# A layer's first output projection, moved behind the queries and written as block products

## Chip, cores and metric

One core of a Trainium2 chip runs the whole program. The metric is the device time of one execution in microseconds (us), and the kernel before was timed three times.

## What is computed

Two layers (DEPTH = 2) are applied to x of 1024 tokens by 1024 channels, in float32. Cut to what matters here:

```python
h = rmsnorm(x, norm_g[l])
z = einsum('bld,de->ble', h, w_in[l])
u_pool, g_pool, u_lru, g_lru, q, k, v, g_attn = split(z)
y_pool = pool_mixer(u_pool, pool_w[l], pool_scale[l]) * silu(g_pool)      # 4 groups of 128 channels
y_lru  = rg_lru_bidir(u_lru, ...) * silu(g_lru)                           # 6 blocks of 128 channels
y_attn = block_attention(rope(rmsnorm(q)), rope(rmsnorm(k)), v) * silu(g_attn)   # 6 heads of 128
x = x + einsum('ble,ed->bld', concatenate([y_pool, y_lru, y_attn]), w_out[l])
```

The last line is the output projection: 2048 channels in, 1024 out. The kernel does it in two parts of eight 128-channel rows of y each: part 0 takes pool groups 0 and 1 and the six LRU blocks, part 1 the rest.

## The kernel before

**Layout and precision.** Activations lie with channels on the 128 partitions and the 1024 tokens along the free dimension. Each matmul operand is kept as two float32r tiles, the rounded value (high) and what is left (low). ScalarE (ACT) or VectorE (DVE) casts the high half, DVE subtracts it for the low one (`split_to`, 518; `fill`, 1012), and `mm3` (544) multiplies high by high, high by low and low by high: three matmuls of 128x128 by up to 512 columns.

**Order of the work.** `record_kernel` (438) writes the operations down layer by layer, and a planner (`Plan.plan`, 303) turns them into one queue for each engine. At each step it takes the operation that can start first by its own costs; among those, the lowest number wins, which is the place in the record less what `ahead(n)` (458) gives. Each engine then runs its queue in order, so an instruction that waits holds all behind it. SyncE (SP) issues the plain DMAs, GpSimd (POOL) the adding ones (`accumulate`, 515) and the `pow` of the norms.

**Buffers.** Tiles belong to groups with a fixed number of buffers (441 to 455): F has 27 of 128x1024, RAW 3 for weights as loaded, WH and WL 2 each for their high and low halves, M 5 of 128x512. A group may have to wait until another is dead (`after`): the attention tiles `at` and `ap` lie where the normalised input `hT` lay, and `st` after them. The same holds in PSUM: a layer has MM, 3 tiles of two banks, and only when all its MM tiles are dead PS, 6 tiles of one bank, in the same place; SG has the two other banks. Buffers of a group are given out in the order of the record, unless enough are free for those that stand earlier.

**A layer** (the loop at 1253): pool groups 0 and 1, six LRU blocks (each two projections of 48 matmuls, gates, scans), pool groups 2 and 3, `out_proj` (966) for part 0, then a gate projection and its silu, k and v (`phase_kv`, 832), q (`phase_q`, 878), four more gate projections, the first three score steps of the attention, the sixth gate projection, and the 48 attention steps (`att_scores`, `att_tr`, `att_pv`). The scores need a PSUM tile of MM, a row maximum on DVE, an exponential on ACT, a reciprocal and a scaling; then TensorE (PE) transposes them.

**Part 0** is a plain product: for each of 8 output tiles, 2 token halves x 8 inputs x 3 matmuls, 384 in all, with 8 weights, 8 x rows and 8 results moved by SP. Its inputs are split as soon as they are made (`lru_gate_out`, 740) and lie in F until then.

**Part 1** is already done by `Fast` (1022) in block products. The eight inputs are two rows of four tiles and the tokens two halves T1 and T2, so y is a 2x2 matrix of blocks. Seven products of each output pair, four inputs x 3 matmuls each, give what eight would: 7 x 4 x 12 = 336. For that, four sums of y blocks (t1 to t4) and, for each pair, two tiles of sums of weight blocks (`weight_sums`, 1069) are needed; the latter are made by adding DMAs in DRAM. `head` and `c11` do the products with B11 and B21 into MM tiles, `run` (1143) first t3, t2 and t4 of every pair, then t1 and B22. In layer 0 the norm of the next layer follows at once: `Norm.finish` (633) for tokens T1 is recorded between those two loops, with `ahead(-LATE)`, and its two small sums use SG.

Of the kernel before, what the change touches and what calls it, by code (L numbers as in the profile page):

```python
# [10 lines left out]
F32 = mybir.dt.float32  # L11
# [5 lines left out]
L = 2  # L17
# [33 lines left out]
DC = 300  # L51
LATE = 50

# [384 lines left out]
def record_kernel(nc, ins, outT):  # L438
# [17 lines left out]
    P.layer = 0  # L456

# [16 lines left out]
    def MM(name="mm"):  # L474
        return P.tile(f"MM{P.layer}", [128, 1024], F32, name)

    def bank(name):
        return P.tile(f"PS{P.layer}", [128, 512], F32, name)

    def SM(name="sm"):  # L480
        return P.tile("SG", [128, 512], F32, name)
# [124 lines left out]
    class Norm:  # L606
        def __init__(self, t0, cols, add="DVE", pool_lo=()):
            self.x = {}
            self.acc = None
            self.t0, self.cols, self.adder, self.pool_lo = t0, cols, add, pool_lo  # L610
            self.ss = SM("ss") if add == "PE" else None
            self.warm = None

        def add(self, xk, k=None):
# [18 lines left out]
        def finish(self, l, hT):  # L633
            t0, nc = self.t0, self.cols // 128
            r = S("nr")[:, 0:nc]
            if self.ss is None:
                ss = SM("ss")
# [12 lines left out]
            if self.warm is not None:  # L650
                self.keep_warm(self.acc, KEEP[1])
            rb = SM("rb")
            for c in range(nc):
# [311 lines left out]

    def out_proj(l, part, y, src, dst, halves, norm=None):
        xn_t = []
        for half in halves:
            t0 = half * HALF if half is not None else 0
            n = Norm(t0, HALF) if norm is not None else None  # L970
            cols = HALF if half is not None else T
            for j in range(NK):
                w = stream_w(wo[l, part, j])
                xr = RAW("xr") if half is None else M("xr")
                P.sync.dma_start(out=xr, in_=src[j][:, t0:t0 + cols])
                if half is None:
                    last = (l, part, j) == (L - 1, 1, NK - 1)
                    mm = MM()
                    parts = TAIL if last else ((0, 512), (512, 1024))
                    for a, b in parts:  # L980
                        for k in range(NK):
                            kk = slice(k * 128, (k + 1) * 128)
                            mm3(mm[:, a:b], w[0][:, kk], w[1][:, kk], y[k][0][:, a:b], y[k][1][:, a:b], k == 0, k == NK - 1)
                    for a, b in parts if last else ((0, T),):
                        P.vector.tensor_tensor(out=xr[:, a:b], in0=xr[:, a:b], in1=mm[:, a:b], op=ALU.add)
                        P.sync.dma_start(out=dst[j][:, a:b], in_=xr[:, a:b])
                else:
                    mm = MM()[:, 0:HALF]
                    proj_half(mm, w, y, half)
                    if half == 0:  # L990
                        xn_t.append(F("xn"))
                    xn = xn_t[j][:, t0:t0 + HALF]
                    P.vector.tensor_tensor(out=xn, in0=xr, in1=mm, op=ALU.add)
                    P.sync.dma_start(out=dst[j][:, t0:t0 + HALF], in_=xn)
                    n.add(xn)
            if n is not None:
                with ahead(-LATE if half == 0 else 0):
                    n.finish(*norm)

# [22 lines left out]
    class Fast:  # L1022
# [67 lines left out]

        def operand(self, src, early, sign=1):
            self.n = getattr(self, "n", -1) + 1
            w = block(("WH", "WL")[self.n % 2], "wf")
            with ahead(early):
                fill(w, src, sign)
            return w
# [46 lines left out]
        def run(self):  # L1143
# [6 lines left out]
            self.c11(*self.todo.pop(0))  # L1150
            tail = []
            for p in pairs:
# [42 lines left out]
        def c12(self, j, b, w):  # L1195
            self.product(b, w, "B22", False)
            self.add(j, T2, b, ALU.add)
            self.done(j, T2)


    P.group("Q2", 2)
    for l in range(L):
        P.group(f"ap{l}", 4, after=f"hT{l}")
    hT = alloc_hT(0)
# [48 lines left out]
    for l in range(L):  # L1253
        P.layer = l
        pw = gate_weights(wp[l])
        yp = []
        if l > 0:
            first = [stream_w(wcm[l, CH_UP]), stream_w(wcm[l, CH_GP])]
            firsts = [MM(), MM()]
            for half in range(2):  # L1260
                for w, ps in zip(first, firsts):
                    proj_half(ps[:, half * HALF:(half + 1) * HALF], w, hT, half)
        prev = pool_group(l, 0, hT, *firsts[0:2])
        cur = pool_group(l, 1, hT, *firsts[2:])
        yp.append(split(pool_out(l, 0, pw, *prev), T, "y"))
        prev = cur

        y = []
        xc = lru_conv(l, 0, proj(l, CH_UL, hT))
        yp.append(split(pool_out(l, 1, pw, *prev), T, "y"))  # L1270
        for j in range(NB):
            if j + 1 < NB:
                nxc = lru_conv(l, j + 1, proj(l, CH_UL + j + 1, hT))
            lru = Lru(l, j, gate_weights(wg[l, j]), *xc)
            lru.gates(0)
            s = silu(proj(l, CH_GL + j, hT))
            lru.gates(1)
            y.append(lru_gate_out(lru.scan(), s))
            xc = nxc
        pw = gate_weights(wp[l])  # L1280
        prev = pool_group(l, 2, hT)
        cur = pool_group(l, 3, hT)
        yp.append(pool_out(l, 2, pw, *prev, True))
        prev = cur
# [17 lines left out]
        def scores(n):  # L1302
# [5 lines left out]
            att_scores(us[i], h, kT, "F" if n < 3 else f"ap{l}")  # L1308
        scores(0)
        ws = Fast.weight_sums(l, 1, us[0].first)  # L1310
        scores(1)
        scores(2)
        sg.append(silu(proj(l, CH_GA + 5, hT, singles()), True))
        for n, (i, h) in enumerate(steps):
# [3 lines left out]
            if i > 0:  # L1318
                att_pv(us[i - 1], v, sg, h, True)
                if h == GQ - 1 and us[i - 1].g == 0 and us[i - 1].c == NT - 1:  # L1320
                    fast = Fast(l, 1, yp[2:] + sg[0:2], sg[2:6], f"st{l}", ws)
                    with ahead(-100):
# [29 lines left out]
def hymba_kernel(ctx: ExitStack, tc: tile.TileContext, *aps):  # L1352
# [12 lines left out]
    def make(t):  # L1365
# [5 lines left out]
        if g == "SG":  # L1371
            return psum.tile(t.shape, t.dtype, tag=f"{g}{t.slot}", name=t.name)
        for of, key, space in ((side, {"hT": "h", "at": "a", "ap": "a", "st": "s"}.get(g[:2]), {}),
                               (banks, {"MM": "m", "PS": "p"}.get(g[:2]), dict(space=bass.MemoryType.PSUM))):
# [86 lines left out]
```

## Time and profile before

| | us |
|---|---|
| median of 3 runs (lowest to highest) | 1629.21 (1627.88 to 1629.31) |
| the profiled execution | 1628.12 |
| its span, first to last instruction | 1626.3 |
| PE busy | 1609.0 (99%) |
| DVE busy | 1108.1 (68%) |
| ACT busy | 789.6 (49%) |
| POOL busy | 113.8 (7%) |

The span lies within the execution's time; the 1.8 us left is around it. Matmuls are pipelined, so that one has a duration of some 0.39 us and the next starts 0.23 us later: what a matmul costs in a full queue is the distance of starts, and a busy PE is one that had a matmul under way. Part 1 of layer 0 runs from 737 to 826 us and that of layer 1 from 1540 us on; part 0 of layer 0 lies within 285 to 400 us, the start of its attention at 551 us.

### The profile page before, as it was taken

The numbers are of one execution on the slowest core, as the hardware profiler recorded it, in microseconds if no ns is written. First come the engines' busy times: TensorE is split into PE (matmuls) and PEld (weight loads), VectorE is DVE, ScalarE is ACT, GpSimd is POOL, SyncE is SP. The second block draws the span as 40 slices with busy tenths as digits, with TensorE's granted clock in tenths as the row PEclk, the third lists the DMA queues.
The fourth block names the chain that finished last, engine by engine and source line by source line (L and its number), as shares of the span: only waits on it lengthen the run. The fifth ranks groups of instructions, "written<-read, shape, count | busy, mean of one in ns | idle before, by whom it ended". The sixth has DMA issues, their size and how long they took to land.

```text
span 1626.3 us, 20051 instructions
## 1 busy us (share of the span) xinstructions
PE 1609.0 (99%) x7878; PEld 1367.7 (84%) x7878; DVE 1108.1 (68%) x1675; ACT 789.6 (49%) x1262; POOL 113.8 (7%) x130
## 2 busy tenths in 40 slices
PE   8999999999999999999999999999999999999999
PEld 8788888888898889998878888888889987999987
DVE  7659889225564489998875688872255635899874
ACT  5357873012332377775342677721133325777731
POOL 1000000000121120101000000000001212101010
PEclk9999999999999999999999999999999999999999
DMA  6110111335111660107331111114431128402172
GB/s 199 39 59 33 59 39 52 127 129 187 37 39 39 181 105 20 33 5 225 113 105 51 46 57 34 62 43 147 155 128 37 40 58 201 76 17 39 32 220 97
DMA packets 51471, 136.87 MB, mean 84 GB/s; under 512 B 5936, under 2 KB 11056, under 8 KB 51248
## 3 DMA queue, kind: packets, MB, share of 16 engines
q1 hardware_dynamic: 41008, 117.88, 21.4%
q0 software_dynamic: 10368, 17.70, 6.9%
q8 instruction: 62, 1.02, 0.3%
q14 instruction: 33, 0.27, 0.1%
HBM read 109.48 MB, written 35.65 MB: 89 GB/s over the span
## 4 chain that ended last, share of the span: by engine, by line
PE 94%; DVE 2%; ACT 1%; issue 1%; DMA 1%; POOL 1%; SPq 0%; ACTq 0%; POOLq 0%
PE mm L430 62%; PE o L430 8%; PE S L430 8%; PE pt L430 5%; PE c L430 3%; PE a L430 3%; PE b L430 3%; PE d L430 1%; POOL ssq L430 1%; PE qtr L430 1%; DMA raw<-wcm 0%; DVE ra L430 0%; DVE hTl L430 0%; SPq L430 0%; DVE sq L430 0%
## 5 line engine op out<-in xcount | busy, mean ns | idle before, releaser
L430 PE MATMUL mm<-hTh,wh 128*128 128x512 f32 x784 | 309.6, 395 | 0.4 <-ACT U L430 0.4
L430 PE MATMUL mm<-hTl,wh 128*128 128x512 f32 x784 | 308.8, 394 | 0.0
L430 PE MATMUL mm<-hTh,wl 128*128 128x512 f32 x784 | 306.6, 392 | 0.0
L430 ACT CAST wh<-raw 128x1024 fp32r<-128x1024 f32 x56 | 58.8, 1050 | 291.4 <-PE mm L430 289.4
L430 PEld LDWEIGHTS mm<-hTh,wh 128*128 128x128 f32 x784 | 147.1, 188 | 35.6 <-ACT U L430 0.9
L430 PEld LDWEIGHTS mm<-hTh,wl 128*128 128x128 f32 x784 | 147.1, 188 | 34.9
L430 PEld LDWEIGHTS mm<-hTl,wh 128*128 128x128 f32 x784 | 147.3, 188 | 32.7
L430 DVE TENSOR_TENSOR wl<-raw,wh 128x1024 fp32r<-128x1024 f32 x65 | 79.2, 1220 | 95.4 <-ACT wh L430 93.1
L430 PE MATMUL mm<-wq,hTh 128*128 128x384 f32 x512 | 133.6, 341 | 0.0
L430 ACT CAST pTh<-pt 128x1024 fp32r<-128x1024 f32 x94 | 94.9, 1012 | 67.2 <-PE pt L430 67.0
L430 DVE TENSOR_TENSOR pTl<-pt,pTh 128x1024 fp32r<-128x1024 f32 x94 | 114.5, 1220 | 15.7 <-ACT pTh L430 15.2
L430 DVE TENSOR_REDUCE st<-S 128x1 f32<-128x1024 f32 x96 | 116.5, 1217 | 3.5 <-PE S L430 3.1
L430 ACT ACTIVATE p<-S,st 128x1024 f32<-128x1024 f32 x96 | 107.5, 1121 | 3.0 <-DVE st L430 3.0
L430 POOL TENSOR_TENSOR ssq<-ssq,mhalf 128x3 f32<-128x3 f32 (+1 forms) x48 | 43.5, 907 | 909.5 <-DVE ssq L430 909.5
L430 DVE TENSOR_TENSOR xr<-xr,mm 128x1024 f32<-128x1024 f32 x16 | 19.5, 1221 | 122.4 <-PE mm L430 122.4
L430 PE MATMUL mm<-yh,wh 128*128 128x512 f32 x256 | 100.8, 394 | 0.0
L430 PE MATMUL mm<-yh,wl 128*128 128x512 f32 x256 | 100.7, 393 | 0.0
L430 PE MATMUL mm<-yl,wh 128*128 128x512 f32 x256 | 100.5, 393 | 0.0
L430 PE MATMUL pt<-ident,p 128*128 128x128 f32 x752 | 97.5, 273 | 0.0
L430 PEld LDWEIGHTS pt<-ident,p 128*128 128x128 f32 x752 | 87.1, 140 | 11.0 <-ACT p L430 1.0
L430 PEld LDWEIGHTS mm<-wq,hTh 128*128 128x128 f32 x512 | 91.5, 189 | 0.0
L430 PE MATMUL o<-pTl,vh 128*128 128x384 f32 x256 | 90.2, 352 | 0.0
(188 smaller groups left out, 3313.0 us busy)
## 6 DMA issues: line engine op xcount, KB each, us to landing
raw<-wcm SPq DMA_DIRECT2D x52, 512.0 KB, 3.8
raw<-wo SPq DMA_DIRECT2D x16, 512.0 KB, 3.9
x<-xr SPq DMA_DIRECT2D x16, 512.0 KB, 2.7
wf<-w SPq DMA_DIRECT2D x16, 512.0 KB, 4.4
xn<-x SPq DMA_DIRECT2D x16, 512.0 KB, 5.5
raw<-wq SPq DMA_DIRECT2D x16, 384.0 KB, 3.3
w<-wo POOLq DMA_DIRECT2D x24, 256.0 KB, 6.8
xr<-xT SPq DMA_DIRECT2D x8, 512.0 KB, 3.7
```

What stands on the lines that cost most here:

```text
L430: getattr(real[op.engine], m)(*[res(x) for x in a], **{n: res(x) for n, x in k.items()})
```

## The change

Part 0 is no longer a plain product. The new class `First` does it in the seven block products of `Fast`, and it runs after q and all gate projections, directly before the attention. The y's go to DRAM as they are made (signed, so that the sums are additions), and the t sums of them are made there by SP copies and POOL adding DMAs; the weight sums of part 0 are made in LRU block 1. What the attention and part 1 need later (pool outputs 2 and 3 and the six silus) is stored to DRAM and loaded again behind `First`. The t blocks lie in a new group `sa`, which waits for `hT` to be dead; `at` and `ap` wait for `sa`. PSUM changes from MM to PS twice in a layer. The first three score steps are recorded inside `First`, before its last product; the sixth gate projection is no longer behind them. In part 1 of layer 0, the operands for t1 and B22 are made in the first loop and held in F, the norm's sums of the first half use PS, and LATE is 20 instead of 50; in both layers the subtraction of the t1 product is recorded with `ahead(60)`.

```diff
-LATE = 50
+LATE = 20
...
+    for i in range(2 * L):
+        P.group(f"MM{i}", 3, after=f"PS{i - 1}" if i else None)
+        P.group(f"PS{i}", 6, after=f"MM{i}")
     for l in range(L):
-        P.group(f"MM{l}", 3, after=f"PS{l - 1}" if l else None)
-        P.group(f"PS{l}", 6, after=f"MM{l}")
         P.group(f"hT{l}", 16, after=f"st{l - 1}" if l else None)
-        P.group(f"at{l}", 4, after=f"hT{l}")
+        P.group(f"sa{l}", 16, after=f"hT{l}")
+        P.group(f"at{l}", 4, after=f"sa{l}")
...
-    def lru_gate_out(h, s):
-        P.vector.tensor_tensor(out=h, in0=h, in1=s, op=ALU.mult)
-        return split(h, T, "y")
+    def lru_gate_out(h, s, signs):
+        for t, sign in zip((T1, T2), signs):
+            P.vector.scalar_tensor_tensor(out=h[:, t], in0=h[:, t], scalar=sign, in1=s[:, t], op0=ALU.mult, op1=ALU.mult)
+        return h
...
@@ Fast.run
+                if self.norm:
+                    w = self.load(self.ws[p][1])
+                    kept.append((self.operand(w[:, T1], 0, 1, "F"), self.operand(w[:, T2], 0, 1, "F")))
             self.c21(*tail.pop())
             if self.norm:
+                self.norms[0].psum = bank
                 with ahead(-LATE):
                     self.norms[0].finish(*self.norm)
             for p in pairs:
-                with ahead(150):
-                    w = self.load(self.ws[p][1])
-                    w1, w4 = self.operand(w[:, T1], 0), self.operand(w[:, T2], 0)
+                if self.norm:
+                    w1, w4 = kept[p]
+                else:
+                    with ahead(150):
+                        w = self.load(self.ws[p][1])
+                        w1, w4 = self.operand(w[:, T1], 0), self.operand(w[:, T2], 0)
                 b = bank("b") if p < 3 else SM("b")
                 self.product(b, w1, "t1", True)
-                self.add(2 * p + 1, T2, b, ALU.subtract)
+                with ahead(60):
+                    self.add(2 * p + 1, T2, b, ALU.subtract)
...
+    class First(Fast):
...
+        def put(self, k, y):
+            P.sync.dma_start(out=self.d[k], in_=y)
+            if k < 4:
+                return
+            i = k - 4
+            x, y, a, b = self.d[i], self.d[k], self.t13[i], self.t24[i]
+            for o, t in ((a[:, T1], x[:, T1]), (a[:, T2], y[:, T2]), (b[:, T1], y[:, T2]), (b[:, T2], y[:, T1])):
+                P.sync.dma_start(out=o, in_=t)
+            for o, t in ((a[:, T1], x[:, T2]), (a[:, T2], x[:, T2]), (b[:, T1], a[:, T1]), (b[:, T2], b[:, T1])):
+                accumulate(o, t)
+
+        def block(self, n, i, early=0):
+            self.B[n][i] = block("F" if n[0] == "B" else self.group, n)
+            with ahead(early):
...
+                fill(self.B[n][i], self.load(a[:, t], M))
...
+        def c11(self, p, a, w):
+            self.product(a, w, "B21", False)
+            self.put_x(2 * p, T1, self.half_x(2 * p, T1), (a, ALU.add))
+
+        def run(self, then):
+            V, A = P.vector, wo[self.l, self.part]
+            pairs = range(NK // 2)
+            for n in ("B11", "B21"):
+                for i in range(4):
+                    self.block(n, i, 100)
+            for n in ("t3", "t1", "t2", "t4"):
+                for i in range(4):
+                    self.block(n, i)
+            self.head(0)
+            for p in pairs[1:]:
+                self.head(p)
+                self.c11(*self.todo.pop(0))
+            self.c11(*self.todo.pop(0))
+            for i in range(4):
+                self.block("B22", i)
+            for p in pairs:
+                j1, j2 = 2 * p, 2 * p + 1
+                c = self.c(p)
+                with ahead(150):
+                    w, w_ = self.load(self.ws[p][0]), self.load(self.ws[p][1])
+                    w3, w1, w2 = self.operand(w[:, T1], 0), self.operand(w_[:, T1], 0), self.operand(w[:, T2], 0)
+                    wa = self.operand(self.load(A[j2][:, T2], M), 0)
+                    w4 = self.operand(w_[:, T2], 0)
+                last = p == len(pairs) - 1
+                c_, b, d = bank("c"), SM("b") if last else bank("b"), SM("d")
+                x2 = F("xr")
+                P.sync.dma_start(out=x2, in_=self.src[j2])
+                self.product(c_, w3, "t3", True)
+                V.tensor_tensor(out=x2[:, T2], in0=x2[:, T2], in1=c_, op=ALU.subtract)
+                self.product(b, w1, "t1", True)
+                V.tensor_tensor(out=x2[:, T2], in0=x2[:, T2], in1=b, op=ALU.subtract)
+                self.product(d, w2, "t2", True)
+                V.tensor_tensor(out=c, in0=c, in1=d, op=ALU.subtract)
+                x23 = x2.rearrange("p (h t) -> p h t", t=HALF)
+                V.tensor_tensor(out=x23, in0=x23, in1=c[:, None, :].to_broadcast([128, 2, HALF]), op=ALU.subtract)
+                P.sync.dma_start(out=self.dst[j2][:, T2], in_=x2[:, T2])
+                self.product(c_, wa, "t4", False)
+                self.put_x(j2, T1, x2[:, T1], (c_, ALU.subtract))
+                if last:
+                    P.banks += 1
+                    then()
+                self.product(b, w4, "B22", False)
+                self.put_x(j1, T2, self.half_x(j1, T2), (c, ALU.add), (b, ALU.add))
...
@@ the loop over layers
-            y.append(lru_gate_out(lru.scan(), s))
+            if j == 1:
+                part0.ws = Fast.weight_sums(l, 0, lru.last)
+            part0.put(2 + j, lru_gate_out(lru.scan(), s, (1.0, -1.0) if j < 2 else (-1.0, 1.0)))
...
-        out_proj(l, 0, yp[:2] + y, xs[l], x1, [None])
-        yp.append(pool_out(l, 3, pw, *prev, True))
-        sg = [silu(proj(l, CH_GA, hT))]
+        keep(pool_out(l, 2, pw, *prev, True))
+        keep(pool_out(l, 3, pw, *cur, True))
+        keep(silu(proj(l, CH_GA, hT)))
...
-        for h in range(1, 5):
-            sg.append(silu(proj(l, CH_GA + h, hT)))
+        for h in range(1, 6):
+            keep(silu(proj(l, CH_GA + h, hT), h == 5))
...
-        scores(0)
+        def start():
+            for n in range(3):
+                scores(n)
+        part0.run(start)
         ws = Fast.weight_sums(l, 1, us[0].first)
-        scores(1)
-        scores(2)
-        sg.append(silu(proj(l, CH_GA + 5, hT, singles()), True))
+        sg = [again(d) for d in kept[2:]]
```

## Rows read from the trace of the kernel before

**Rows 1.** Page: busy time of the engines, then the granted clock in 40 slices

```profile
PE 1609.0 (99%) x7878; PEld 1367.7 (84%) x7878; DVE 1108.1 (68%) x1675; ACT 789.6 (49%) x1262; POOL 113.8 (7%) x130
...
PEclk9999999999999999999999999999999999999999
```

**Rows 2.** Page: chain that ended last, shares of the span by engine

```profile
PE 94%; DVE 2%; ACT 1%; issue 1%; DMA 1%; POOL 1%; SPq 0%; ACTq 0%; POOLq 0%
```

**Rows 3.** Windows: us, busy of PE, PEld, DVE, ACT, POOL; clock, DMA share, GB/s

```profile
60.00:290.00 230.00, 230.00 (x995) 186.53 (x994) 184.72 (x167) 141.33 (x144) 0.00 (x0) 1.00 0.16 52
290.00:370.00 80.00, 80.00 (x348) 64.90 (x347) 17.51 (x15) 7.36 (x7) 0.00 (x0) 1.00 0.40 137
758.00:764.00 6.00, 6.00 (x28) 4.85 (x27) 5.11 (x11) 3.74 (x7) 0.00 (x0) 1.00 0.92 330
765.00:797.00 32.00, 32.00 (x139) 25.76 (x138) 25.42 (x39) 8.75 (x14) 0.00 (x0) 1.00 0.50 182
1538.00:1567.00 29.00, 29.00 (x137) 24.42 (x136) 22.63 (x46) 15.37 (x27) 7.83 (x9) 1.00 0.86 225
```

**Rows 4.** Groups by line and form: part 0's products, and operations that the change adds

```profile
L430 PE MATMUL mm<-yh,wh 128*128 128x512 f32 x256 | 100.8, 394 | 0.0
...
L430 DVE TENSOR_TENSOR wf<-wf 128x512 fp32r<-128x512 f32 x48 | 33.1, 691 | 8.5 <-ACT wf L430 8.2
...
L430 DVE TENSOR_TENSOR yl<-gate,yh 128x1024 fp32r<-128x1024 f32 x12 | 14.7, 1225 | 0.0
...
L430 DVE TENSOR_TENSOR xn<-xn,c 128x512 f32<-128x512 f32 x16 | 10.9, 683 | 6.9 <-PE c L430 6.9
...
L430 DVE TENSOR_TENSOR xn<-xn,p 128x1024 f32<-128x1024 f32 x8 | 9.8, 1219 | 0.0
```

**Rows 5.** Chain in order of time: start, us, count of matmuls

```profile
58.55 344.67 PE mm L430 x1488
...
769.03 5.59 PE c L430 x24
```

**Rows 6.** Timeline of PE and DVE, end of layer 0: start, us, count, idle before

```profile
812.52 2.94 PE L430 MATMUL b<-t,wf 128*128 128x512 f32 x12
818.79 7.38 PE L430 MATMUL b<-B,wf 128*128 128x512 f32 x24 [3.33 <-DVE xn L430]
...
814.03 0.74 DVE L430 SCALAR_TENSOR_TENSOR xn<-xn,vecs,rb 128x512 f32<-128x512 f32 x1
...
817.96 0.68 DVE L430 TENSOR_TENSOR xn<-xn,b 128x512 f32<-128x512 f32 x1
```

**Rows 7.** Windows, end of layer 0 (columns as in rows 3)

```profile
797.00:840.00 43.00, 39.67 (x182) 32.35 (x181) 34.89 (x61) 18.57 (x30) 2.05 (x2) 0.96 0.35 122
...
818.80:822.00 3.20, 3.20 (x10) 2.53 (x11) 2.84 (x5) 2.33 (x5) 0.00 (x0) 0.67 0.53 200
```

**Rows 8.** Timeline, start of layer 0's attention: PE, ACT, DVE

```profile
551.39 0.40 PE L430 MATMUL S<-kTh,qh 128*128 128x512 f32 x1
...
555.37 1.28 ACT L430 ACT_TABLE_LOAD   x1 [2.47 <-DVE st L430]
...
558.11 0.75 DVE L430 TENSOR_SCALAR p<-p,st 128x1024 f32<-128x1024 f32 x1
...
566.88 1.03 PE L430 MATMUL pt<-ident,p 128*128 128x128 f32 x8
...
572.71 0.47 PE L430 MATMUL S<-kTh,qh 128*128 128x512 f32 x1 [1.65 <-DVE pTl L430]
...
576.37 0.42 PE L430 MATMUL o<-pTh,vh 128*128 128x384 f32 x1
```

**Rows 9.** DMA issues: median us to landing; an adding DMA's time on POOL

```profile
xn<-x SPq DMA_DIRECT2D x16, 512.0 KB, 5.5
...
t1f<-sg SPq DMA_DIRECT2D x8, 256.0 KB, 2.3
...
L430 POOL DMA_DIRECT2D w<-wo x24 | 20.5, 881 | 114.9 <-DMA w<-wo 76.6 <-issue 38.3
```

More of the change, by code (lines that the diff above doesn't have):

```diff
@@ L449, in record_kernel @@
     P.group("SG", 2)
+    for i in range(2 * L):
+        P.group(f"MM{i}", 3, after=f"PS{i - 1}" if i else None)
+        P.group(f"PS{i}", 6, after=f"MM{i}")
     for l in range(L):
-        P.group(f"MM{l}", 3, after=f"PS{l - 1}" if l else None)
-        P.group(f"PS{l}", 6, after=f"MM{l}")
         P.group(f"hT{l}", 16, after=f"st{l - 1}" if l else None)
-        P.group(f"at{l}", 4, after=f"hT{l}")
+        P.group(f"sa{l}", 16, after=f"hT{l}")
+        P.group(f"at{l}", 4, after=f"sa{l}")
         P.group(f"st{l}", 12, after=f"at{l}")
-    P.layer = 0
+    P.banks = 0
     class ahead:
@@ L474, in MM @@
     def MM(name="mm"):
-        return P.tile(f"MM{P.layer}", [128, 1024], F32, name)
+        return P.tile(f"MM{P.banks}", [128, 1024], F32, name)
     def bank(name):
-        return P.tile(f"PS{P.layer}", [128, 512], F32, name)
+        return P.tile(f"PS{P.banks}", [128, 512], F32, name)
     def SM(name="sm"):
@@ L963, in att_pv @@
                 P.vector.tensor_tensor(out=y[:, t], in0=y[:, t], in1=o[:, h * 128:(h + 1) * 128], op=ALU.mult)
[L966 to L998, printed above, removed]
     def block(group, name):
@@ L1089, in load, with operand @@
             return w
-        def operand(self, src, early, sign=1):
-            self.n = getattr(self, "n", -1) + 1
-            w = block(("WH", "WL")[self.n % 2], "wf")
+        def operand(self, src, early, sign=1, group=None):
+            if group is None:
+                self.n = getattr(self, "n", -1) + 1
+            w = block(group or ("WH", "WL")[self.n % 2], "wf")
             with ahead(early):
@@ L1150, in run @@
             self.c11(*self.todo.pop(0))
-            tail = []
+            tail, kept = [], []
             for p in pairs:
@@ L1198, in c12, with __init__, half_x, put_x @@
             self.done(j, T2)
+    class First(Fast):
+        def __init__(self, l, src, dst):
+            self.l, self.part, self.group = l, 0, f"sa{l}"
+            self.B = {n: [None] * 4 for n in ("B11", "B21", "B22", "t1", "t2", "t3", "t4")}
+            self.src, self.dst, self.todo = src, dst, []
+            self.d, self.t13, self.t24 = [[P.tile("dram", [128, T], F32, f"{n}{l}{k}") for k in range(c)]
+                                          for n, c in (("yd", NK), ("t13_", 4), ("t24_", 4))]
+        def put(self, k, y):
[11 more added lines that the diff above has]
+            with ahead(early):
+                a, t = {"B11": (self.d[i], T1), "B21": (self.d[4 + i], T1), "B22": (self.d[4 + i], T2),
+                        "t1": (self.t13[i], T1), "t3": (self.t13[i], T2), "t2": (self.t24[i], T1),
+                        "t4": (self.t24[i], T2)}[n]
+                fill(self.B[n][i], self.load(a[:, t], M))
+        def half_x(self, j, t, tile=M):
+            x = tile("xr", cols=HALF)
+            P.sync.dma_start(out=x, in_=self.src[j][:, t])
+            return x
+        def put_x(self, j, t, x, *adds):
+            for what, op in adds:
+                P.vector.tensor_tensor(out=x, in0=x, in1=what, op=op)
+            P.sync.dma_start(out=self.dst[j][:, t], in_=x)
+        def c11(self, p, a, w):
[45 more added lines that the diff above has]
+                self.put_x(j1, T2, self.half_x(j1, T2), (c, ALU.add), (b, ALU.add))
@@ L1201, in record_kernel @@
     P.group("Q2", 2)
     for l in range(L):
-        P.group(f"ap{l}", 4, after=f"hT{l}")
+        P.group(f"ap{l}", 4, after=f"sa{l}")
     hT = alloc_hT(0)
@@ L1253, in record_kernel @@
     for l in range(L):
-        P.layer = l
+        P.banks = 2 * l
         pw = gate_weights(wp[l])
-        yp = []
         if l > 0:
@@ L1262, in record_kernel @@
                     proj_half(ps[:, half * HALF:(half + 1) * HALF], w, hT, half)
+        part0 = First(l, xs[l], x1)
         prev = pool_group(l, 0, hT, *firsts[0:2])
         cur = pool_group(l, 1, hT, *firsts[2:])
-        yp.append(split(pool_out(l, 0, pw, *prev), T, "y"))
+        part0.put(0, pool_out(l, 0, pw, *prev, True))
         prev = cur
-        y = []
         xc = lru_conv(l, 0, proj(l, CH_UL, hT))
-        yp.append(split(pool_out(l, 1, pw, *prev), T, "y"))
+        part0.put(1, pool_out(l, 1, pw, *prev, True))
         for j in range(NB):
@@ L1277, in record_kernel, with keep, again @@
             lru.gates(1)
-            y.append(lru_gate_out(lru.scan(), s))
+            if j == 1:
+                part0.ws = Fast.weight_sums(l, 0, lru.last)
+            part0.put(2 + j, lru_gate_out(lru.scan(), s, (1.0, -1.0) if j < 2 else (-1.0, 1.0)))
             xc = nxc
+        def keep(y):
+            d = P.tile("dram", [128, T], F32, f"kept{l}_{len(kept)}")
+            kept.append(d)
+            P.sync.dma_start(out=d, in_=y)
+        def again(d):
+            y = F("yk")
+            P.sync.dma_start(out=y, in_=d)
+            return y
+        kept = []
         pw = gate_weights(wp[l])
@@ L1320, in record_kernel @@
                 if h == GQ - 1 and us[i - 1].g == 0 and us[i - 1].c == NT - 1:
-                    fast = Fast(l, 1, yp[2:] + sg[0:2], sg[2:6], f"st{l}", ws)
+                    fast = Fast(l, 1, [again(d) for d in kept[:2]] + sg[0:2], sg[2:6], f"st{l}", ws)
                     with ahead(-100):
@@ L1372, in make @@
             return psum.tile(t.shape, t.dtype, tag=f"{g}{t.slot}", name=t.name)
-        for of, key, space in ((side, {"hT": "h", "at": "a", "ap": "a", "st": "s"}.get(g[:2]), {}),
+        for of, key, space in ((side, {"hT": "h", "sa": "f", "at": "a", "ap": "a", "st": "s"}.get(g[:2]), {}),
                                (banks, {"MM": "m", "PS": "p"}.get(g[:2]), dict(space=bass.MemoryType.PSUM))):
```

7 lines of the change are left out of this document (3 added, 4 removed).

## Prediction

> **What bounds the kernel now.** The page comes first: PE is busy for 1609.0 of 1626.3 us, the next engine, DVE, for 1108.1, and the granted clock stands in its top tenth in all 40 slices [rows 1]. The chain that ended last has 94% of its length on PE [rows 2]. The windows by stage show that this is no mean over unlike stages: from 60 to 290 us, in part 0 (290 to 370) and in both runs of part 1, PE is busy all the time [rows 3]. So time goes only where matmuls go, or where PE already waits, and each other engine matters only if it makes PE wait. PE's whole idle time is 1626.3 - 1609.0 = 17.3 us; only a few of these can be had.
>
> **What a matmul costs.** Its duration is 394 ns [rows 4], but they overlap. In full queues the starts lie 344.67 / 1488 = 0.2316 us apart, and in block products 5.59 / 24 = 0.233 [rows 5]; I take 0.232.
>
> **The change, part by part.** The sum is made against the profiled execution, 1628.1 us, which is 1.1 below the median of 1629.2.
>
> *Matmuls removed.* Part 0 has 768 matmuls in both layers (256 in each of three groups, of which one is shown [rows 4]). Seven products of 4 x 3 for 4 pairs are 336 a layer, 672 in all. 96 fewer at 0.232 are -22.3 us. The stage shrinks from 89.1 to 78.0 us a layer. Nothing else is added on PE.
>
> *End of layer 0.* PE waits there once: the matmuls of 812.52 end at 815.5, and the next, at 818.79, waits 3.33 us for a subtraction (`xn<-xn,b`) that DVE starts at 817.96, behind the norm's multiplications [rows 6]. After it the granted clock is 0.67, between the levels of 2.4 and 1.2 GHz [rows 7], and 24 matmuls take 7.38 instead of 24 x 0.233 = 5.59 us, 1.8 more. So 5.1 us are there to be had. The eight operands made earlier take 8 x 0.69 = 5.5 us of lows [rows 4] out of a stretch where DVE is busy for 34.9 of 43 us [rows 7], and the subtraction is put ahead. Bounds: 0 to -5.1. I take -4.5, nearly all: the first loop must take the 5.5 us in, and it has 32.0 - 25.4 = 6.6 us free [rows 3]. Late next would be the second half of the norm, covered by the next layer's 48 matmuls on the first half (11.1 us).
>
> *Inside the new stage.* DVE has, per layer, 20 blocks made after `hT` is dead and 28 weight operands, at 0.69 each 33.1 us; four results of the head at 0.68, 2.7; and per pair six subtractions and additions of 512 columns, 6 x 0.68, and one of 1024 columns at 1.22, so 21.2 for four [rows 4]. That is 57 of 78 us, 73%; in the head alone 16 blocks, 8 operands and 4 results, 19.3 of 22.3 us. Part 1 runs at 79% (25.42 of 32) without a PE wait [rows 3]. DMA is tighter: in pieces of 256 KB, 20 blocks, 8 + 16 + 4 of weights, 16 of x and 16 results are 80, or 21.0 MB in 78 us: 269 GB/s. Part 1 moved 182 and 225; over 6 us 330 was reached [rows 3]. SP's some 64 issues leave it room. PSUM changes hands twice: at the first, the last `c11` product (2.8 us) covers an eviction of 0.68; at the second, the B22 product does. Bounds: a gain is excluded, since PE has no idle time in part 0 to give back; above, two waits of the size just seen, 2 x 5.1 a layer. Nearest are the windows of part 1, with none. I take 1.5 a layer for the fuller DMA: +3.0.
>
> *Start of the attention.* Three score steps are followed today by the 48 matmuls of the sixth gate projection, up to 566.88 us, which hide their softmax; PE waits 1.65 us in all [rows 8]. That cover goes. From the first score matmul (551.39) to a scaled p (558.86) are 7.5 us; 1.28 of them load a table, which now comes after the last silu, and DVE is late by some 1.1, since a silu's multiplication stands ahead of the first maximum: its tile is done at 551.39 + 6 x 0.233 = 552.8, and with 0.2 to get there and 1.22 for 1024 columns [rows 4] ACT could start at 554.2 instead of 555.37. So 5.1 are left, and the three steps fill 18 x 0.233 = 4.2. From the first transposition (566.88) to the first o (576.37) are 9.5 us, with 1.65 idle among them. So PE would wait 0.9 + 1.65, up to 3.3 + 1.65 if the softmax gets no faster, and then perhaps lose 1.8 to the clock. Against today that is between -1.65 (no wait left) and +5.1. I take +1.3 a layer, near the first working since its two savings have rows: +2.6.
>
> *Moved work, at nothing.* In the LRU blocks the low half (1.225) goes and a multiplication becomes two halves, some 0.3 more; PE has no wait there to lose [rows 3]. Stores of y, copies for the sums (16 a layer) and the weight sums (12) go past SP's weight loads, which run a projection (11.1 us) ahead; without that lead each would delay a projection by its landing, 2.3 us [rows 9]. The 16 + 20 adding DMAs at 0.88 us, 32 us, stand on POOL, which does nothing from 60 to 290 us [rows 9, 3]; behind them is the first `pow` of k, five projections (56 us) after the last. Were that gone, k's norm would wait for them. Without the long part 0 ahead of it, k and v's weights are prepared beside those five projections. The silus loaded again are needed only with the first output, over 20 us after the scores start; they land in 5.5 us [rows 9], in a window that the weight sums of part 1 also fill. Each cover is several times what it hides; if the reload's failed, DVE, and behind it the whole softmax, would wait.
>
> **Sum.** -22.3 - 4.5 + 3.0 + 2.6 = -21.2, so 1606.9, said as 1607.
>
> **The rivals.**
>
> *A, nothing new is lost.* No wait in the new stage and the whole tail gained: 1628.1 - 22.3 - 5.1 = 1600.7, and 1597.4 if the wait of 1.65 goes too. For it: part 1 has the same structure and no wait. Against it: the lost cover. Chance 0.12.
>
> *B, the tail does not change.* The operands are made early but the planner still sets the norm's work before the subtraction: the change does not do this part. 1607 + 4.5 = 1611.5. Against it: `ahead(60)` aims at just that instruction. Chance 0.08.
>
> *C, the handovers are felt.* Attention at its upper bound (+7.6 over my sum) gives 1614.5, the stage at its bound too (2 x 5.1 instead of 1.5 a layer, +17.4) 1632; between them, one handover a layer at 5.1 (+7.2) gives 1621.7. For it: 16 blocks have five M buffers, and x for `c11` stands behind them. Chance 0.13, most of it below 1622.
>
> *D, DMA sets the pace: slower.* Part 0 fetched whole rows; now blocks of 256 KB come one for each 0.98 us, and one alone takes 2.3 us to land [rows 9]. Were the stage held to the 225 GB/s of the longest busy window [rows 3], its 21.0 MB would take 93.3 us instead of 78.0: +30.6, less the 3.0 counted, gives 1634.5. It decides below 233 GB/s: there the stage takes 90.1 us, and 12.1 more a layer eat the -22.3 - 4.5 + 2.6. Against it: 330 GB/s for 6 us in just such transfers, and part 1's 182 GB/s at half the DMA share [rows 3]. Chance 0.05. The Trainium skill, "DMA: Bandwidth & Descriptors", in its section on bandwidth, speaks for D: it says to batch transfers to 1 MiB or more for three quarters of the peak. By its fit of 2.0 us plus bytes over 436 GB/s, 256 KB taken one by one would get some 100 GB/s, an estimate of over 200 us for this stage. This trace does not bear that out where several are under way: 330 GB/s stands in rows 3.
>
> **How the numbers follow.** My own case, 1602 to 1612, has 0.60; 0.02 is left for no change. A difference under 0.2%, 3.3 us, can hardly be told from none. Faster: 0.60 + 0.12 + 0.08 + 0.13 = 0.93; slower 0.05. The range 1600 to 1618 leaves out about half of A (0.06), D, no change, and the part of C above 1618 (0.06): 0.19.
>
> **What would show it.** Right: 96 fewer matmuls; PE full in the new stage with block products 0.233 us apart; no wait for `xn<-xn,b` at the end of layer 0 and a granted clock of 1.00 there; a wait of 2 to 3 us behind the first scores. Wrong: matmuls of `First` that wait for DVE blocks or DMA (C, D), a DMA share near 1 over the stage, a clock below 1.00 at a layer's attention start, the old wait at the tail (B), or a wait in the LRU blocks, k or q, where I count nothing.

## The result, and the profile after

The median of four runs is 1615.20 us (1612.52 to 1616.12), against 1629.26 us of four runs of the kernel before: a ratio of 0.9909, with an interval of 0.9894 to 0.9925. That is 14.1 us less, where 22 had been forecast: inside the range of 1600 to 1618, outside my own case of 1602 to 1612. The profiled execution took 1612.52 us, the shortest of the four; its span is 1610.7 us, 15.6 less than before.

The page of the changed kernel: busy time, granted clock in 40 slices, the chain's shares by engine, and the products of the new stage (`c` and `a`) among the groups.

```profile
PE 1589.8 (99%) x7782; PEld 1349.1 (84%) x7782; DVE 1164.3 (72%) x1817; ACT 822.3 (51%) x1344; POOL 171.7 (11%) x202
...
PEclk9999999999999999999999999999999999999999
...
PE 92%; DVE 3%; DMA 2%; ACT 2%; issue 1%; SPq 0%; POOL 0%; POOLq 0%; ACTq 0%; DVEq 0%
...
L430 PE MATMUL c<-t,wf 128*128 128x512 f32 x384 | 93.9, 395 | 0.3 <-DVE xr L430 0.3
L430 PE MATMUL a<-B,wf 128*128 128x512 f32 x384 | 90.6, 395 | 0.9 <-ACT p L430 0.9
```

Against [rows 1] and [rows 2]: exactly 96 matmuls fewer, PE still busy nearly all the time, but its part of the chain fell from 94% to 92%. Work of other engines has come into the chain, and the question is where. (A slice of the clock row is 40 us long; a few us at a lower clock do not show in it.)

The windows of the changed kernel, columns as in [rows 3]: the new stage of layer 0 as a whole, its fullest 10 us for DMA, the same stage of layer 1, and the end of layer 0.

```profile
480.00:557.00 77.00, 76.26 (x327) 60.92 (x326) 54.99 (x86) 28.54 (x48) 0.00 (x0) 1.00 0.78 277
...
500.00:510.00 10.00, 9.70 (x43) 7.51 (x42) 5.78 (x9) 2.58 (x5) 0.00 (x0) 1.00 1.03 407
...
1272.00:1350.00 78.00, 77.58 (x334) 62.28 (x333) 56.00 (x88) 28.65 (x48) 0.00 (x0) 1.00 0.79 279
...
785.00:830.00 45.00, 45.00 (x212) 37.04 (x211) 37.23 (x65) 15.69 (x25) 2.03 (x2) 1.00 0.30 106
```

In these windows PE loses 0.74 us in the stage of layer 0 and 0.42 in that of layer 1, at a DMA rate of 277 and 279 GB/s, where the sum had 269. At the end of layer 0 PE is busy for all of 45 us at a clock of 1.00: the wait of [rows 6] and the slow clock of [rows 7] are gone.

The waits of PE in the changed kernel: what waited for what, us in total, times, longest.

```profile
PE mm L430 <- DVE sg L430: 7.9, 6, 2.8
...
PE S L430 <- DVE pTl L430: 1.2, 2, 0.6
...
PE a L430 <- ACT p L430: 0.9, 2, 0.4
```

The same view of the kernel before:

```profile
PE b L430 <- DVE xn L430: 3.3, 1, 3.3
PE S L430 <- DVE pTl L430: 3.3, 2, 1.7
```

The first row of the changed kernel had no counterpart before. `mm<-DVE sg` is a matmul of a pool group's output or of a projection that waits for the scaling of the pool group's gate. It falls at two places, and the timeline shows both. First place, the output of pool group 0 in layer 0; one row of PE before the wait, the row with it, and the scaling on DVE:

```profile
70.77 0.40 PE L430 MATMUL mm<-pmh,gwh 128*128 128x512 f32 x1
72.01 0.50 PE L430 MATMUL mm<-pml,gwh 128*128 128x512 f32 x1 [0.84 <-DVE sg L430]
...
71.20 0.75 DVE L430 SCALAR_TENSOR_TENSOR sg<-mm,vecs,sg 128x512 f32<-128x512 f32 x1 [1.16 <-PE mm L430]
```

The output of a pool group is one tile over two banks, one for each half of the columns. The scaling is now two instructions, and the planner set the first of them among the matmuls of the second half. It starts at 71.20, when the second half's first matmul (70.77) has ended, and the second half's next matmul starts when it is done: 0.84 us, though the two touch different banks. Both waits are for semaphores: the one that the scaling waits for is raised by the matmul of 70.77, the one that the next matmul waits for by the scaling. So the program itself orders the two, by the tile and not by its banks; what the chip would do without that, no run shows. This wait comes for pool groups 0 and 1 in both layers, four times.

Second place, the last microseconds before k and v's projections in layer 0, as the chain that ended last, in order of time (start, us, what):

```profile
261.96 12.94 PE mm L430 x56
...
274.92 7.75 DMA raw<-wkv
...
282.69 1.05 ACT wkv L430
...
283.77 1.01 DVE wkv L430
...
284.91 1.23 DVE ws L430
...
287.19 1.22 DVE ws L430
288.42 1.13 DVE wkv L430
...
289.71 1.79 DVE sg L430 x2
291.49 1.15 DVE ws L430
...
293.76 12.33 PE mm L430 x52
```

A piece of k and v's weights lands 7.75 us after its issue. ACT's cast waits for it, DVE's low half waits for the cast, and behind that in DVE's queue stand the window sums of pool group 3 (`ws`) and the scaling of pool group 2 (`sg`). PE waits 2.8 us for that scaling, and 1.8 in layer 1. The scaling has nothing to do with those weights.

By stages, from the starts of matmuls in PE's timeline of both profiled executions, both layers together, each row good to some 0.1 us. In the attention's row the products that stand among its first matmuls are taken out.

| stage | prediction | measured |
|---|---|---|
| part 0: 88.8 us before, 79.5 and 78.9 after | -22.3 + 3.0 | -19.2 |
| second run of part 1 in layer 0: 89.2 to 84.1 | -4.5 | -5.1 |
| attention, first score to part 1 | +2.6 | -0.8 |
| pool groups 0 and 1: 13.9 to 16.1 in each layer | 0 | +4.4 |
| output of pool group 2 to the start of k: 13.9 to 17.5 and 16.5 | 0 | +6.2 |
| q, its first matmul to the next projection: 74.0 to 72.8 and 72.9 | 0 | -2.3 |
| the rest, by difference | 0 | +1.2 |
| span | -21.2 | -15.6 |

The gain in q was not looked into further; one of its waits, for `ra`, fell from 1.4 to 0.4 us.

### The profile page after: what moved, and what is told of

The parts are those of the page before. It is cut to its first block, busy times and chain, and to the rows that moved or that the text cites. A ratio compares the mean times of both kernels' runs of the same rounds, so it can differ in the third digit from the quotient of the medians.

```text
span 1610.7 us, 20655 instructions
## 1 busy us (share of the span) xinstructions
PE 1589.8 (99%) x7782; PEld 1349.1 (84%) x7782; DVE 1164.3 (72%) x1817; ACT 822.3 (51%) x1344; POOL 171.7 (11%) x202
## 4 chain that ended last, share of the span: by engine, by line
PE 92%; DVE 3%; DMA 2%; ACT 2%; issue 1%; SPq 0%; POOL 0%; POOLq 0%; ACTq 0%; DVEq 0%
PE mm L430 52%; PE o L430 8%; PE S L430 8%; PE c L430 6%; PE b L430 5%; PE pt L430 5%; PE a L430 4%; PE d L430 3%; DMA raw<-wkv 1%; PE qtr L430 1%; DMA xr<-xT 0%; DVE sg L430 0%; DVE ws L430 0%; DMA raw<-wcm 0%; DVE pTl L430 0%
## 5 line engine op out<-in xcount | busy, mean ns | idle before, releaser
L430 ACT CAST wf<-wf 128x512 fp32r<-128x512 f32 x86 | 52.6, 621 | 171.2 <-PE c L430 44.4
L430 ACT CAST wh<-raw 128x1024 fp32r<-128x1024 f32 x46 | 48.3, 1051 | 151.2 <-PE mm L430 143.1
L430 DVE TENSOR_TENSOR wl<-raw,wh 128x1024 fp32r<-128x1024 f32 x49 | 59.3, 1217 | 70.7 <-ACT wh L430 70.7
L430 PE MATMUL c<-t,wf 128*128 128x512 f32 x384 | 93.9, 395 | 0.3 <-DVE xr L430 0.3
L430 PE MATMUL a<-B,wf 128*128 128x512 f32 x384 | 90.6, 395 | 0.9 <-ACT p L430 0.9
L430 PE MATMUL o<-pTh,vh 128*128 128x384 f32 x256 | 90.2, 352 | 0.4 <-DVE pTl L430 0.4
L430 PEld LDWEIGHTS c<-t,wf 128*128 128x128 f32 x384 | 72.0, 188 | 18.2 <-DVE xr L430 0.7
```

The lines of the kernel that those rows point to most:

```text
L430: getattr(real[op.engine], m)(*[res(x) for x in a], **{n: res(x) for n, x in k.items()})
```

## The experiments

Theory: the missing time is moved work that the prediction put at nothing, in the two places just shown. Rivals: the DMA of the new stage, or the start of the attention. Where the expectations name M and N, N puts a loss on the new transfers and M on the order of work. Medians of the kernel before were 1629.86 us in the first four experiments, 1629.63 in the next four and 1629.73 in the last four.

**1. The scaling after all matmuls of its output** (changed kernel, one edit):

```
+        last = P.ops[-1]
...
-            P.vector.scalar_tensor_tensor(...)
+            P.follow(P.vector.scalar_tensor_tensor(...), last)
```

> The changed kernel, with the two scalings of a pool output ordered behind all six of its matmuls. Theory M (the shortfall comes from the scaling in halves: the second half's matmuls wait until DVE has read the first half of the same PSUM tile): the four waits after pool groups 0 and 1, 0.84 us each with some 0.25 around it, go: -4.4 us, and the waits of 2.8 and 1.8 us before k and v shrink, unless another takes their place: 1606 to 1611 us. Rival N (DMA of the moved sums and of the k and v weights is late, and DVE and ACT with it): 0 to -4.4, with the waits before k and v as long as they were.

Measured: 1614.75 us, 0.9909 (0.9894 to 0.9924), the same as the change. The waits of PE in this kernel:

```profile
PE mm L430 <- DVE sg L430: 7.3, 2, 4.3
```

Two waits instead of six: the four of 0.84 are gone and pool groups 0 and 1 take 13.9 us again, as before the change. But the two ahead of k grew from 2.8 and 1.8 to 4.3 and 3.0, and k starts at 304.28 us instead of 303.84: M's 1606 to 1611 is missed. What is gained early in a layer is waited for before k. In layer 0 PE goes on at 290.37 us, where it went on at 290.42 in the changed kernel, since the chain from the weights' DMA ends no earlier.

The longer wait also has a price of its own. The windows behind it, in the changed kernel and here (columns as in [rows 3], the clock is the third number from the end):

```profile
291.00:294.00 3.00, 2.71 (x12) 1.92 (x11) 2.54 (x4) 1.34 (x2) 0.00 (x0) 1.00 0.31 112
```

```profile
291.00:294.00 3.00, 3.00 (x9) 2.32 (x8) 1.75 (x3) 0.83 (x1) 0.00 (x0) 0.50 0.14 57
```

Behind 2.8 us of waiting the granted clock was 1.00, behind 4.3 us it was 0.50, and 0.50 again behind the 3.0 us of layer 1 (1083 to 1086 us). There matmuls start 0.427 us apart instead of 0.233, eight of them in layer 0 and some seven in layer 1: an estimate of 3 us. So the two losses stand in series, one hides the other, and the clock takes more than the rest.

**2. The end of layer 0 alone** (kernel before, with the tail's edits only):

```
+                self.norms[0].psum = bank
...
+                if self.norm:
+                    w = self.load(self.ws[p][1])
+                    kept.append((self.operand(w[:, T1], 0, 1, "F"), self.operand(w[:, T2], 0, 1, "F")))
...
+                with ahead(60):
+                    self.add(2 * p + 1, T2, b, ALU.subtract)
```

> The kernel before with only the edits at the end of layer 0 (operands for t1 and B22 made in the first loop, norm's sums in PS, LATE 20, the subtraction put ahead). Theory: the wait of 3.33 us and the slow matmuls behind it, 1.8 us, go: -5.1, 1624.1 us. Rival: the tail is gained only because the rest of the change moved other work: 0, 1629.

Measured over ten runs: 1625.44 us, 0.9977 (0.9968 to 0.9986), or -4.4 us. The row `PE b <- DVE xn` is gone from the waits. This part of the change does what it says, by itself.

**3. The scaling in halves alone** (kernel before, unsigned outputs scaled in two halves):

```
-   ... if signed else ((slice(0, T), col(l, V_PS + g)),):
+   ... if signed else ((T1, col(l, V_PS + g)), (T2, col(l, V_PS + g))):
```

> The kernel before with the scaling of pool outputs 0 and 1 in two halves and nothing else. Theory M: two waits of some 1.1 us a layer appear, +4.4 us, 1633.6. Rival (the waits come from the stores of y or from other work that the change moves there): 0, 1629.

Measured over ten runs: 1633.73 us, 1.0021 (1.0012 to 1.0031), or +3.9 us. The waits of PE show the first place, without any transfer of the change:

```profile
PE mm L430 <- DVE sg L430: 3.4, 4, 0.8
```

So the halves cost 3.9 us of their own where no later wait takes them up.

**4. No sums of y** (experiment 1, and the blocks of part 0 loaded from the y tiles themselves). It leaves out the sums and differences of y, so that part 0 multiplies other numbers; every matmul and load stays:

```
-            for o, t in (...): P.sync.dma_start(out=o, in_=t)
-            for o, t in (...): accumulate(o, t)
+            self.t13[i], self.t24[i] = x, y
```

> As e1_scale_after_all, with the sums of y left out: no copies and no adding DMAs for t13 and t24, the t blocks are loaded from the y tiles themselves, so part 0 is computed from wrong sums. Theory M: within 2 us of e1, and before k and v nothing changes but what DMA share there was. Rival N: 4 to 6 us below e1, since the DMA of the sums makes the k and v weights late.

Measured: 1605.82 us, 0.9854 (0.9839 to 0.9869), 8.9 less than experiment 1. The waits ahead of k fall to 1.2 each. What changed is the landing of k and v's weights. The four pieces of layer 0 in the changed kernel, then here (issued 2.6 us earlier, at the same distances):

```profile
DMA to landing us min/median/max: 4.3/6.6/7.8
```

```profile
DMA to landing us min/median/max: 3.6/4.0/4.5
```

M falls for this place, and N holds, by more than it asked: sums of the last y run while k and v's weights come in. In the changed kernel's trace its copies had landed by 274.7 us; what is under way beside the three late pieces, issued from 274.92 us on, are two adding DMAs of 256 KB, which took 8.3 and 9.7 us to land. The stretch from 270 to 285 us has a DMA share of 0.80 at 239 GB/s in the changed kernel, 0.68 at 206 here, and 0.11 at 36 in the kernel before, so the mean share alone does not tell the late landing from the early one.

**5. The last y's sums behind q** (experiment 1, nothing left out: the sums of the last of the eight are recorded after q and follow its last `pow` on POOL):

```
-            if k < 4:
-                return
+            if 4 <= k < 7:
+                self.sums(k)
...
+        part0.sums(7, <last POOL operation of q>)
```

> As e1_scale_after_all (1614.8), with the sums of the last y (its four copies and four adding DMAs) recorded behind q and waiting for the last pow of q. Theory (those transfers run beside the k and v weights, one weight then lands 7.8 us after its issue instead of some 4, and DVE, which waits for it in order, brings the scaling of pool output 2 late): the waits of 4.3 and 3.0 us before k and v fall to the 1.2 of e5_no_y_sums: 1606 us, with nothing left out. Rival (the sums cost by their amount, wherever they stand, or POOL's queue gets late in q): 1612 to 1615.

Measured: 1605.68 us, 0.9857 (0.9842 to 0.9871), the same as experiment 4, with waits of 1.2 and 1.2. It is the last y alone that does the harm, and that by its place in time.

**6. k and v's weights later** (experiment 1, and the planner asked to prepare them 60 us later):

```
-        w = load_w_piece(wkv[l], 512, "wkv")
+        with ahead(-60):
+            w = load_w_piece(wkv[l], 512, "wkv")
```

> As e1_scale_after_all, with the loading and splitting of the k and v weights given 60 places less priority. Theory (the wait is one of DVE's order: work on pool groups 2 and 3 stands behind a weight that is not there): the wait before k and v falls by 2 to 4 us a layer, unless k itself then waits for its weights: 1607 to 1612. Rival (DMA amount alone): the weights land later still, and k waits as long as pool output 2 did: 1614 or more.

Measured: 1605.26 us, 0.9859 (0.9842 to 0.9875). The y sums stay where they were, and two pieces of the weights still land 7.6 and 7.7 us after their issue in layer 0; yet nearly the same is won: PE waits 0.8 and 0.4 in layer 0 and not at all in layer 1. A transfer that lands late costs little by itself here; it costs because other work stands behind it in DVE's queue.

**7. The exponential's table not loaded ahead** (experiment 1; the last silu is not followed by an exponential):

```
-            keep(silu(proj(l, CH_GA + h, hT), h == 5))
+            keep(silu(proj(l, CH_GA + h, hT)))
```

> As e1_scale_after_all, without the small exponential that loads ACT's table after the last silu. By the prediction's working of the attention start (a saving of 1.28 on the softmax): +1.3 us a layer, 1617.4. Rival (the table load hides beside the last product and the three score steps): 0.

Measured: 1622.56 us, 0.9955 (0.9940 to 0.9970), 7.8 more than experiment 1, but not where it was looked for. The load of 1.28 us is back ahead of the first softmax, at 565.47, and the stretch from the first score to part 1 takes 175.90 us, against 175.81 in experiment 1: there it costs nearly nothing. The time went to other places (`c <- DVE xr` 3.5 us in the new stage, `mm <- DVE sg` 9.0 instead of 7.3). Part of it is the clock, which reads 0.50 from 290 to 295 us, behind a wait of 5.2 us before k. One operation less seems to have given the planner another order for much of the layer; both expectations are missed, and for the 7.8 us as a whole the run is inconclusive.

**8. More DMA in the new stage** (experiment 1, with eight more copies of 512 KB in DRAM per layer, from the first product of the stage on):

```
+            for k in range(NK):
+                more = P.tile("dram", [128, T], F32, f"more{self.l}{k}")
+                P.follow(P.sync.dma_start(out=more, in_=self.d[k]), first)
```

> As e1_scale_after_all, with eight more copies of 512 KB from DRAM to DRAM, beginning with the first product of the new stage: 4.2 MB more, read and written, on a stage that moves 277 GB/s at a DMA share of 0.78. Rival D (the stage runs at what DMA can give): +5 to +12 us a layer, since the stage is full. Mine (it has room: PE loses 0.7 us in it): 0 to +3 a layer.

Measured: 1648.03 us, 1.0112 (1.0097 to 1.0127), 33.3 more than experiment 1 and beyond both expectations. Its waits of PE, first row, and its windows in the stage of layer 0:

```profile
PE c L430 <- DVE xr L430: 25.4, 2, 14.1
```

```profile
490.00:500.00 10.00, 10.00 (x44) 8.09 (x44) 6.03 (x10) 4.53 (x8) 0.00 (x0) 1.00 1.00 406
500.00:510.00 10.00, 6.75 (x28) 4.81 (x26) 4.35 (x9) 3.10 (x5) 0.00 (x0) 0.98 0.98 356
510.00:520.00 10.00, 0.00 (x0) 0.00 (x0) 3.22 (x6) 1.24 (x2) 0.00 (x0) 0.50 0.98 387
520.00:530.00 10.00, 8.95 (x28) 7.10 (x29) 5.43 (x9) 3.33 (x6) 0.00 (x0) 0.67 0.76 258
```

One wait in each layer, 14.1 and 11.4 us: the head's result waits in PSUM for a half of x that it is to be added to, and the next `c` product needs those banks. PE stands still from 510 to 520 and then runs at a granted clock of 0.67.

**9. Both orders, the best version** (experiments 5 and 6 together):

> e6_last_sums_late and e7_kv_weights_later together. Theory (both take away the same wait of pool output 2 behind a late weight): hardly more than either alone, 1603 to 1606 us. Rival (each removes a loss of its own): 9 us more, 1597.

Measured: 1603.03 us (1601.70 to 1606.26), 0.9839 (0.9823 to 0.9856): faster than both kernels, 12.2 us under the change. Its waits of PE have no `mm <- DVE sg` at all; of the rows shown of the changed kernel these are left:

```profile
PE S L430 <- DVE pTl L430: 1.2, 2, 0.6
...
PE a L430 <- ACT p L430: 0.9, 2, 0.4
```

From the output of pool group 2 to k are 13.9 us in each layer, as before the change. Its step over experiment 6 (2.2 us) is within the scatter of both.

**10. x in another group of buffers** (experiment 6, and the half of x for the head's results taken from `F` instead of `M`):

```
-            self.put_x(2 * p, T1, self.half_x(2 * p, T1), (a, ALU.add))
+            self.put_x(2 * p, T1, self.half_x(2 * p, T1, F), (a, ALU.add))
```

> e7_kv_weights_later with the x halves of the head's results loaded into F tiles instead of M tiles, where they stand behind the sixteen t blocks. Theory (the one tight place of the new stage is that the first c product waits for the PSUM handover, and that for a late x): its wait of 0 to 1.2 us goes, and runs scatter less: 1603 to 1605 us. Rival (nothing is late there as a rule): 1605.3 as before.

Measured: 1605.46 us, 0.9853 (0.9837 to 0.9868), the same as experiment 6. The wait `c <- DVE xr` is gone, but it was 0.4 us there.

**11. Only k and v's weights later** (changed kernel with experiment 6's edit, the scaling as changed):

> The changed kernel (scalings of a pool output as it has them) with the k and v weights 60 places later, nothing else. Theory M: the four waits in pool groups 0 and 1 cost their 4.4 us as soon as nothing behind them waits anyway: 1609.7 us. Rival (e1 showed no gain because they cost nothing): 1605.3.

Measured: 1609.37 us, 0.9875 (0.9855 to 0.9895), 5.8 under the change and 4.1 over experiment 6. Its waits of PE:

```profile
PE mm L430 <- DVE sg L430: 4.2, 5, 0.8
```

With the second place cleared, the first is paid in full: 4.1 us between the medians (their ranges overlap), 3.9 in experiment 3. Four of the five waits, 3.4 us, stand there.

**12. More DMA, with x in the other group** (experiment 8 with experiment 10's edit; one run):

> e9_more_dma with the x halves of the head's results in F tiles. If its 33 us come from x alone (waits of 14.1 and 11.4 us of the first c product), these waits fall below 3 us each and the time to 1620. Rival D (the stage then has more to move than DMA can give, whichever piece is last): a product with t blocks waits instead, and the time stays above 1635.

Measured: 1625.14 us, between the two expectations. Two of the rows of PE's waits over the whole run, and windows of layer 0's stage as in experiment 8:

```profile
PE c L430 <- DVE xr L430: 3.1, 1, 3.1
PE b L430 <- ACT wf L430: 1.5, 1, 1.5
```

```profile
490.00:500.00 10.00, 10.00 (x44) 8.07 (x43) 6.66 (x11) 3.99 (x7) 0.00 (x0) 1.00 1.01 379
...
510.00:520.00 10.00, 9.42 (x30) 7.48 (x31) 5.06 (x9) 3.19 (x6) 0.00 (x0) 0.69 1.04 415
```

Some 23 of the 33 us went with one tile's place. The halves of x share their buffers with 16 blocks of y's sums, and in `F` the wait falls from 25.4 us to 3.1. The other 10 us are spread: the rows of PE's waits add up to 20.4 us, against 16.3 in experiment 1, and behind the waits the clock is low (0.69 from 510 to 520 us). The transfers run at 379 to 415 GB/s with a share of about 1; that this is their limit is not shown. The extra copies also wait in SP's queue for the stage's first product; that was not tried apart.

## Why the prediction was right and wrong

**The matmuls: right.** 96 fewer, and the stage 9.3 and 9.9 us shorter. The 3.0 us for its DMA came out in size: 79.5 and 78.9 us against the 78.0 of the sum leave 1.5 and 0.9 us. Of these PE's idle time in the windows is 0.74 and 0.42; that DMA is the cause is not shown. Rival D was wrong for this change, since 277 GB/s is over its 233, and the fullest 10 us reached 407. With 4.2 MB more a layer (experiment 8) the stage of layer 0 has 14 us of waiting PE, but most of that went with the place of x (experiment 12). The fit in the Trainium skill, "DMA: Bandwidth & Descriptors", section "Anatomy of one DMA", is for one DMA. The estimate of some 100 GB/s from it, for pieces one by one, does not hold where many are under way: this stage moved 277 GB/s.

**The end of layer 0: right.** I took -4.5 of 5.1; the trace has -5.1, and the part alone -4.4. So rival B falls. In the changed kernel's DVE timeline the subtractions stand between the norm's multiplications, and PE never waits for one.

**The attention's start: wrong in sign.** I took +2.6 and the trace has -0.8. The changed kernel's timeline, PE from the first score, and ACT's table load and scaling of the first softmax:

```profile
557.00 0.39 PE L430 MATMUL S<-kTh,qh 128*128 128x512 f32 x1
...
561.19 1.80 PE L430 MATMUL b<-B,wf 128*128 128x512 f32 x7
562.83 1.03 PE L430 MATMUL pt<-ident,p 128*128 128x128 f32 x8
...
569.34 0.50 PE L430 MATMUL S<-kTh,qh 128*128 128x512 f32 x1 [0.60 <-DVE pTl L430]
...
482.80 1.28 ACT L430 ACT_TABLE_LOAD   x1
...
561.47 1.15 ACT L430 ACTIVATE p<-p,st 128x1024 f32<-128x1024 f32 x1
```

From the first score to a scaled p are 5.6 us (557.00 to 562.62), where I had 5.1 of the 7.5 in [rows 8]. What I missed stands on PE. Seven matmuls of the last `B22` product lie behind the scores, and 18 + 7 of them at 0.233 fill 5.8 us. I had counted that product as over when the scores began. The wait of 1.65 became 0.60. The table's 1.28 us were a right row for the wrong term: experiment 7 puts the load back ahead of the softmax, without a loss there.

**The moved work, at nothing: the step that failed.** It is +10.6 us: one term was left out, and one cover failed.

The term left out: "a multiplication becomes two halves, some 0.3 more; PE has no wait there to lose" speaks of the LRU outputs, and no wait of PE stands in the LRU blocks. But the change scales pool outputs 0 and 1 in halves too (`pool_out` with `signed`), and the prediction has no word on that. The first half's scaling stands among the second half's matmuls, and these wait for it, 0.84 us each of four times (experiments 1, 3 and 11). That PE had no wait in these stages [rows 3] says nothing of a wait that the edit itself makes.

The cover that failed: "Without the long part 0 ahead of it, k and v's weights are prepared beside those five projections". That is where they are prepared, and I named no price if the cover failed. In the same stretch run the y sums that I had counted on POOL (32 us, "which does nothing") and past SP, but not on the DMA engines. I took the landing of a load as 2.3 us [rows 9], a row of 256 KB pieces; those of k and v, of 512 KB, took 3.4 to 4.4 us in the kernel before and up to 7.8 beside the sums, and the preparation stands in DVE's queue ahead of a scaling that PE needs. Experiments 4, 5 and 6 each take away one link (the traffic, its time, the place in the queue), and each is about 9 us (8.9 to 9.5) faster than experiment 1. Some 3 us of that are the clock behind experiment 1's longer waits, which none of the three has; against the changed kernel the place is worth 5.8 us (experiment 11).

The sum with these terms: 1606.9 + 10.6 (moved work) - 3.4 (attention) - 0.6 (tail) + 0.1 (stage) - 2.3 (q) + 1.2 (rest) = 1612.5, the profiled execution's time; it closes because the rest is taken by difference. The changed median lies 2.7 higher: the profiled run was the fastest of four, at a mean clock of 0.998, and the others have 0.996 or 0.997.

**The rivals.** C named handovers in the stage and at the attention; its size (1614.5 to 1632) came true and its place did not. A needed nothing new lost: it gave 1600.7, and experiment 9, which loses nearly nothing new, has 1603.0.

**Luck.** That the median lies within 1600 to 1618 owes something to chance. The moved work alone would have put the profiled execution at 1606.9 + 10.6 = 1617.5 and the median, 2.7 higher, past the range; the attention (-3.4) and q (-2.3) brought it back, and I had foreseen neither.

## What to carry to other kernels

Where each engine works through a fixed queue, a late transfer is paid by whatever stands behind the work that waits for it, so ask of each moved load not only when it lands but what is queued behind its first use. When an eviction over two banks is cut in halves, look at which matmuls stand between the halves in the order. Two waits in series mask each other: curing the first alone gained nothing here, since PE went on at the same microsecond and then ran some 3 us at the lower clock; curing the second alone gained 5.8 us, and curing both some 10.

## What the runs showed of the hardware

Loads of 512 KB, issued at the same distances, landed in 3.6 to 4.5 us without the sums of y (experiment 4) and in 4.3 to 7.8 us beside adding DMAs within DRAM, at mean DMA shares of 0.68 and 0.80. With PE idle from 510 to 520 us in experiment 8 the granted clock read 0.50, and 0.67 in the next 10 us. Behind a wait of PE of 2.8 us it stayed at 1.00 (changed kernel); behind waits of 3.0 and 4.3 us it was 0.50 for some 3 us (experiment 1). DMA moved up to 415 GB/s over 10 us.
